# Low parts of every second weight unit on GpSimd from a2's keys to the output projection's first half, with the heads' scales one step and C's products two steps later

## The chip, the cores and the metric

The kernel runs on one core of a Trainium2 chip. The metric is the device time of one execution in microseconds (us), and the time of a kernel is the median of several runs. The engines are TensorE (PE; its weight loads are PEld), VectorE (DVE), ScalarE (ACT), GpSimd (POOL) and SyncE (SP), which here only issues DMAs.

## The reference

One decoder layer on x of 512 tokens and 2048 channels, in float32. A first RMSNorm and one input projection make the inputs of three token mixers, whose outputs go through one output projection and are added to x; then come a second RMSNorm and a SwiGLU block, added again.

```
proj = rms_norm(x) @ w_in                        # 2048 -> 3840 columns
A: 8 heads x 64, dilated sliding windows (128,1), (512,4), (2048,16), mixed by their softmax sums
B: u * sigmoid(gate) -> causal depthwise conv, 31 taps -> LayerNorm -> silu, 512 channels
C: 16 query heads x 64 over 2 kv heads, window 128, one learned sink per head
x  = x + concat(A, B, C) @ w_out                 # 2048 -> 2048
h2 = rms_norm(x)
x  = x + (silu(h2 @ w_gate) * (h2 @ w_up)) @ w_down
```

A and C normalise queries and keys per head before the scores.

## The kernel before, in words

**Products in three parts.** A float32 operand is split into a high part, the operand rounded to the matmul's type, and a low part, what the rounding left. Every product of a weight tile with the activations is then three matmuls (`mm3`, L321 to L324): high by high, high weights by low activations, low weights by high activations. The third one is the only reader of the low weights `wl`.

**Weight units.** The weights come in units of 128x1024. The input projection uses units 0 to 62: a projection's name in `PROJ` (such as `ak2`, the keys of A's head pair 2) takes two units from the fifth name on, and `ak2` begins with unit 35. The output projection takes units 63 to 94, its first half 63 to 78. `split_up_to` makes the parts two units ahead of their use: ACT casts the unit into the high part `wh` (L289), and a later subtraction of `wh` from the raw weights makes `wl` (recorded at L290; the profile puts it at L263, the helper that calls it). Which engine subtracts is the third field of the unit's entry in `works`; in the kernel before it is DVE for all 95 units.

```python
works.append((u, True, nc.vector))                                            # L167
(nc.vector.tensor_copy if u == 0 else nc.scalar.copy)(hi[:, :n], t[:, :n])    # L289
lows.append((eng.tensor_sub, lo[:, :n], t[:, :n], hi[:, :n].bitcast(F32)))    # L290
```

The raw weights, `wh` and `wl` each lie in SBUF. High and low parts have three buffers each, so the cast of unit u waits until PE has done with unit u-3. The raw buffer is given to a later load one unit after the subtraction was recorded.

**Steps.** The order of the work around the projections is set by `Ticks`: a list of functions that are due a number of steps later. A projection ticks after every second weight tile, that is after six matmuls (`project`, L538 to L550); the output projection's first half does the same, its second half ticks half as often. Every engine works through its instructions in the order in which they were recorded, so a function that is due one step later stands six matmuls later in PE's order and behind one more step of other work on DVE, ACT and POOL.

**Heads.** `head_scales` (L622) computes a projection's per-head scales: squares on ACT, a transposed sum on DVE, a small DRAM round trip on SP's queue, and three small operations on POOL (L655 to L657). Keys go on through a DVE transpose (L702), another round trip and a split; their tiles end in `wide`, `k`, `hi`, `lo`. `attention` (L793) then places a head: scores on PE (L814, L815), softmax on DVE and ACT, the flip (PE transposes of the weights: L850 in C, L916 in A), high and low parts of the flipped weights (ACT L856 and DVE L861 in C; ACT L922 and DVE L927 in A), and the products with the values (`weigh`, L940 with the high parts, L941 with the low parts). In C the flipped weights hold two blocks each, and POOL writes them apart with affine selects: `ph` from the high part, `pl` from the low one (L870, L873). `SD` enters only the earliest step of a head's scores:

```python
box["q at"] = ticks.now + SD + 3                                              # L668
return head_scales(b, name, then, home), ticks.now + SD + KD + 10             # L717, a key's step
t0 = max(ticks.now + ready, head_at[0], box["q at"] - s1, box["k at"], box["v at"] - at_v)   # L961
```

`C_TICKS` and `A_TICKS` hold a head's distances in steps, the last one (`we`) that from the split of the flipped weights to their products. A's heads are soft-maxed at L880 to L900 on DVE: the last operation before a flip is L900, which writes `a0e`, `a1e` and so on.

**Beside the heads** run the convolution's 31 taps for each of four channel tiles on DVE (L573, two SBUF inputs), one every 1.2 to 1.6 steps, and in the output projection the residual additions on DVE (`xr`, L1073), which also free the PSUM bank of an output tile; there are two such banks. POOL has, besides, the convolution's gate product (L564) and the scaling of values (L764).

**Later stages.** The SwiGLU block follows with its own order: weight sums on POOL (L172), low parts on DVE (L285, one input in PSUM), and products on PE (L1279 to L1282, L1544 to L1546).

Of the kernel before, what the change touches and what calls it, by code (L numbers as in the profile page):

```python
# [36 lines left out]
T_GLU = 14  # L37


SD, KD, VD, EV = 9, 6, 12, 1  # L40


C_TICKS = (1, 6, 2, 2, 2, 3, 5, 1, 4)
A_TICKS = (0, 8, 2, 1, 3, 1, 3, 1, 5)


PROJ = ("bu0 bg0 bu1 bg1 cv ck cq0 bu2 cq3 cq1 cq5 bu3 cq2 bg2 cq7 "
        "bg3 ak2 cq4 ak0 av0 cq6 ak1 aq0 av1 aq1 ak3 av2 aq2 av3 aq3").split()
ROWS = "c0 c1 c2 c4 c5 c3 c7 c6 a0 a1 b2 b1 b0 b3 a2 a3".split()

N_SLOTS = 73
# [65 lines left out]
def kernel(ctx: ExitStack, tc: tile.TileContext, xT, wi, wo, wgu, wd, cst_in, outT):  # L117
    nc = tc.nc
# [30 lines left out]
    entries, works = [], []  # L149
# [14 lines left out]

    for u, unit in enumerate(units):
        entries.append((RAW_PLAIN[(u - 2) % len(RAW_PLAIN)], u, [unit]))
        works.append((u, True, nc.vector))  # L167

    def plus(to, a, b, n, buf=None):
        def go():  # L170
# [622 lines left out]
    def attention(kind, box, mix, mi, heads):  # L793
        ready, every, step, s1, sx, s2, fl, ev, we = C_TICKS if kind == "c" else A_TICKS

        if mi in ROWS[-2:]:
            fl, we = fl + 2, we + 3
# [217 lines left out]
    ticks.after(t_ln + 12, ln_out, mix)  # L1015
    for n, row in enumerate(r for r in ROWS if r[0] == "b"):
        ticks.after(t_ln + 13 + n, split_mix, row)
# [4 lines left out]
    for name in PROJ[HEAD4:]:  # L1022
        kind, what, j = name[0], name[1], name[2:]
        if name == PROJ[-2]:
            for n, row in enumerate(ROWS[:8]):
                ticks.after(6 + n, split_mix, row)
# [27 lines left out]
    def load_x(i):  # L1054
        if i < KT:
            n = OUT_ORDER[0][i]
            xr[n] = slot(f"xr{n}")
            nc.sync.dma_start(xr[n], xT[n])
# [68 lines left out]
    late.append(True)  # L1127
    for n, row in enumerate(r for r in ROWS if r in mix and r not in m_hi):
        ticks.after(10 + 2 * n, split_mix, row)
    for half in range(2):  # L1130
        for i, n in enumerate(OUT_ORDER[half]):
# [4 lines left out]
            for kk in range(8):  # L1136
                k = 8 * half + kk
                row = ROWS[k]
                while row not in m_hi:
# [6 lines left out]
            if half == 0:  # L1146
                load_x(i + 2)
        for row in ROWS[8 * half:8 * half + 8]:
            if half == 0:
# [544 lines left out]
```

## Time and profile before

| | |
|---|---|
| median of 3 runs | 1844.88 us (1844.69 to 1844.89) |
| the profiled execution | 1845.39 us, of which 1843.6 us are the profile's span |
| PE busy | 1835.2 us (100% of the span) |
| DVE, ACT, POOL busy | 1445.8, 1312.1, 1026.2 us |
| granted TensorE clock | 1.0 over the span |
| chain that ended last, by engine | PE 95%, DVE 3%, DMA 1% |

In order of time the span has the input projection with the heads (to about 389 us), the output projection (to about 580 us), the SwiGLU block's first products (to about 1418 us) and its second ones. A row of the timeline gives an instruction's start, its duration, engine, line, operation and operands; in square brackets stands how long its engine was idle before it and what ended that. A matmul's row is longer than the distance to the next one, since they overlap: the distance from start to start tells whether PE was held up. A row of the waits gives the waiting instruction, what it waited for, the total, the number of times and the longest.

### The profile page before, as it was taken

What the parts mean: (1) busy time and instruction counts of PE and PEld (TensorE: products, weight loads), DVE (VectorE), ACT (ScalarE), POOL (GpSimd) and SP (SyncE); (2) the same over time, 40 slices, a digit from 0 to 9 for tenths busy, and PEclk for the clock granted to TensorE, in tenths of its full rate; (3) what the DMA queues carried; (4) which work ended last, traced back from release to release, by engine and by line L of the source; (5) the groups of instructions that cost most, each with busy time, mean ns of one, the idle gap of its engine ahead of it and who ended that gap; (6) DMA issues with size and microseconds to landing.
All of it is one profiled execution on the core that took longest, in us unless ns stands there. A gap on an engine that the chain in (4) does not pass through costs nothing.

```text
span 1843.6 us, 26502 instructions
## 1 busy us (share of the span) xinstructions
PE 1835.2 (100%) x8314; PEld 1522.4 (83%) x8314; DVE 1445.8 (78%) x2063; ACT 1312.1 (71%) x1784; POOL 1026.2 (56%) x790
## 2 busy tenths in 40 slices
PE   9999999999999999999999999999999999999998
PEld 7888888888888888888888888888888888888887
DVE  6789988997689877778777787777777777777777
ACT  6345554553458788888888888888887778777775
POOL 0126644110003557886788767878676558776552
PEclk9999999999999999999999999999999999999999
DMA  7353345353343457677867778677687679877735
GB/s 276 87 150 93 87 121 153 107 161 116 124 149 103 115 151 191 188 213 182 225 187 200 201 188 226 181 209 199 182 273 258 204 225 295 257 254 260 240 119 110
DMA packets 398924, 334.61 MB, mean 181 GB/s; under 512 B 184256, under 2 KB 326720, under 8 KB 398784
## 3 DMA queue, kind: packets, MB, share of 16 engines
q1 hardware_dynamic: 398208, 332.14, 62.3%
q8 instruction: 66, 1.08, 0.3%
q10 hardware_dynamic: 576, 0.79, 0.1%
q14 instruction: 74, 0.61, 0.1%
HBM read 258.46 MB, written 65.98 MB: 176 GB/s over the span
## 4 chain that ended last, share of the span: by engine, by line
PE 95%; DVE 3%; DMA 1%; issue 0%; ACT 0%; SPq 0%; POOL 0%; DVEq 0%; POOLq 0%; ACTq 0%
PE out L1281 15%; PE out L1279 15%; PE out L1282 15%; PE out L1544 7%; PE out L1546 7%; PE out L1545 7%; PE o L322 3%; PE o L323 3%; PE o L324 3%; PE cq L322 2%; PE cq L324 2%; PE cq L323 2%; PE in L324 1%; PE in L323 1%; PE in L322 1%; PE aq L322 1%
## 5 line engine op out<-in xcount | busy, mean ns | idle before, releaser
L1279 PE MATMUL out<-wh,h 128*128 128x512 f32 x1232 | 479.2, 389 | 0.0
L1281 PE MATMUL out<-wl,h 128*128 128x512 f32 x1232 | 479.2, 389 | 0.0
L1282 PE MATMUL out<-wh,h 128*128 128x512 f32 x1232 | 479.2, 389 | 0.0
L1279 PEld LDWEIGHTS out<-wh,h 128*128 128x128 f32 x1232 | 231.2, 188 | 48.1
L1282 PEld LDWEIGHTS out<-wh,h 128*128 128x128 f32 x1232 | 231.2, 188 | 48.0
L1281 PEld LDWEIGHTS out<-wl,h 128*128 128x128 f32 x1232 | 231.2, 188 | 47.9
L1545 PE MATMUL out<-wl,a 128*128 128x512 f32 x620 | 240.4, 388 | 0.1
L1544 PE MATMUL out<-wh,a 128*128 128x512 f32 x620 | 240.4, 388 | 0.0
L1546 PE MATMUL out<-wh,a 128*128 128x512 f32 x620 | 240.3, 388 | 0.0
L289 ACT CAST wh<-w 128x1024 fp32r<-128x1024 f32 (+2 forms) x94 | 96.9, 1031 | 121.6 <-PE o L323 48.0
L1554 DVE TENSOR_TENSOR y<-y,out 128x512 f32<-128x512 f32 x192 | 128.5, 684 | 47.8 <-PE out L1546 46.1
L263 DVE TENSOR_TENSOR wl<-w,wh 128x1024 fp32r<-128x1024 f32 (+2 forms) x95 | 115.0, 1211 | 30.9 <-ACT wh L289 27.9
L1545 PEld LDWEIGHTS out<-wl,a 128*128 128x128 f32 x620 | 116.4, 188 | 24.5 <-DVE wl L285 0.5
L1546 PEld LDWEIGHTS out<-wh,a 128*128 128x128 f32 x620 | 116.4, 188 | 23.8
L1544 PEld LDWEIGHTS out<-wh,a 128*128 128x128 f32 x620 | 116.4, 188 | 23.8
L573 DVE SCALAR_TENSOR_TENSOR y<-bu,cst,y 128x511 f32<-128x511 f32 (+14 forms) x120 | 92.0, 767 | 1.3
L322 PE MATMUL o<-mh_c,wh 128*128 128x512 f32 x128 | 51.1, 399 | 0.2 <-DVE xr L1073 0.2
L322 PE MATMUL cq<-hh,wh 128*128 128x512 f32 x128 | 50.3, 393 | 0.0
L324 PE MATMUL o<-mh_c,wl 128*128 128x512 f32 x128 | 50.0, 391 | 0.0
L323 PE MATMUL o<-ml_c,wh 128*128 128x512 f32 x128 | 50.0, 390 | 0.0
L323 PE MATMUL cq<-hl,wh 128*128 128x512 f32 x128 | 49.9, 390 | 0.0
L324 PE MATMUL cq<-hh,wl 128*128 128x512 f32 x128 | 49.9, 390 | 0.0
(2351 smaller groups left out, 4766.5 us busy)
## 6 DMA issues: line engine op xcount, KB each, us to landing
od<-a SPq DMA_DIRECT2D x154, 256.0 KB
a<-od SPq DMA_DIRECT2D x154, 256.0 KB
w<-in_wi SPq DMA_DIRECT2D x58, 512.0 KB
w<-in_wo SPq DMA_DIRECT2D x32, 512.0 KB
x<-in_xT SPq DMA_DIRECT2D x16, 256.0 KB
xr<-in_xT SPq DMA_DIRECT2D x16, 256.0 KB
x2d<-xr SPq DMA_DIRECT2D x16, 256.0 KB
z<-x2d SPq DMA_DIRECT2D x64, 64.0 KB
```

Of the source, the lines that this page charges most:

```text
L263: fn(*args)
L289: (nc.vector.tensor_copy if u == 0 else nc.scalar.copy)(hi[:, :n], t[:, :n])
L322: nc.tensor.matmul(out, wh, xh, start=start, stop=False)
L323: nc.tensor.matmul(out, wh, xl, start=False, stop=False)
L324: nc.tensor.matmul(out, wl, xh, start=False, stop=stop)
L1279: nc.tensor.matmul(b, x[:, high], wh[:, s], start=c == f == 0 and q in (7, 1, 5, 2), stop=False, skip_group_check=True)
L1281: nc.tensor.matmul(b, x[:, high], wl[:, s], start=False, stop=False, skip_group_check=True)
L1282: nc.tensor.matmul(b, x[:, low], wh[:, s], start=False, stop=c == f == 1, skip_group_check=True)
L1544: nc.tensor.matmul(b[:, lo:hi], x[:, high], wh[:, s], start=start, stop=False, skip_group_check=True)
L1545: nc.tensor.matmul(b[:, lo:hi], x[:, high], wl[:, s], start=False, stop=False, skip_group_check=True)
L1546: nc.tensor.matmul(b[:, lo:hi], x[:, low], wh[:, s], start=False, stop=last, skip_group_check=True)
L1554: getattr(eng, op)(t, t, src)
```

## The change

Units 35, 37 and so on to 77, which are 22 of the 44 units from the first of `ak2` to the last of the output projection's first half, get their low part from GpSimd instead of VectorE. `SD` becomes 10, so that scores are placed one step later after their projection. The last distance of `C_TICKS` becomes 6, so that C's products stand two more steps behind the split.

```diff
-SD, KD, VD, EV = 9, 6, 12, 1
+SD, KD, VD, EV = 10, 6, 12, 1
-C_TICKS = (1, 6, 2, 2, 2, 3, 5, 1, 4)
+C_TICKS = (1, 6, 2, 2, 2, 3, 5, 1, 6)
+POOL_LOWS = (35, 79)
...
-        works.append((u, True, nc.vector))
+        works.append((u, True, nc.gpsimd if POOL_LOWS[0] <= u < POOL_LOWS[1] and u % 2 else nc.vector))
```

One line is added above all others that the text names, so lines from L49 on have a number one higher in the changed kernel (L263 becomes L264).

Three places show what moves. On PE, at the products of head pair 1 of C (`c1o`), the six rows ahead and the first of the products, before:

```order
L322 MATMUL cq_1740<-hh_410,wh_1674 128x512
L323 MATMUL cq_1740<-hl_411,wh_1674 128x512
L324 MATMUL cq_1740<-hh_410,wl_1675 128x512
L322 MATMUL cq_1740<-hh_435,wh_1674 128x512
L323 MATMUL cq_1740<-hl_436,wh_1674 128x512
L324 MATMUL cq_1740<-hh_435,wl_1675 128x512
L940 MATMUL c1o_1867<-c1ph_1790,cv_745 128x256
L941 MATMUL c1o_1867<-c1pl_1803,cv_745 128x256
```

and now:

```order
L323 MATMUL bg_1885<-hh_160,wh_1728 128x512
L324 MATMUL bg_1885<-hl_161,wh_1728 128x512
L325 MATMUL bg_1885<-hh_160,wl_1729 128x512
L323 MATMUL bg_1885<-hh_186,wh_1728 128x512
L324 MATMUL bg_1885<-hl_187,wh_1728 128x512
L325 MATMUL bg_1885<-hh_186,wl_1729 128x512
L941 MATMUL c1o_1918<-c1ph_1786,cv_745 128x256
L942 MATMUL c1o_1918<-c1pl_1808,cv_745 128x256
```

The products stood in the projection `cq2` and now stand in the next one, `bg2`: 18 projection matmuls later, of which 6 come from `SD` (scores and flip moved by them too) and 12 from `C_TICKS`. Every head of C moved in this way; A's scores, flips and products moved by 6 as long as projections run.

On POOL, at the second head of C's pair 2, the end of its high parts `c2ph`, its low parts `c2pl`, and the scale of the keys `ak2`, before:

```order
L870 AFFINE_SELECT c2ph_2376<-c2hp_2356 128x2x128
L873 AFFINE_SELECT c2ph_2376<-c2hp_2356 128x128
L870 AFFINE_SELECT c2pl_2398<-c2lp_2371 128x2x128
L873 AFFINE_SELECT c2pl_2398<-c2lp_2371 128x2x128
L870 AFFINE_SELECT c2pl_2401<-c2lp_2371 128x2x128
L873 AFFINE_SELECT c2pl_2401<-c2lp_2371 128x128
L695 MEMSET ak2wide 128x24
L655 TENSOR_TENSOR ak2wide<-ak2t 128x8
```

and now:

```order
L871 AFFINE_SELECT c2ph_2383<-c2hp_2354 128x2x128
L874 AFFINE_SELECT c2ph_2383<-c2hp_2354 128x128
L264 TENSOR_TENSOR wl_2365<-w_1914,wh_2364 128x1024
L696 MEMSET ak2wide 128x24
L656 TENSOR_TENSOR ak2wide<-ak2t 128x8
L657 TENSOR_TENSOR ak2wide<-ak2wide,c_531 128x8
L658 TENSOR_TENSOR ak2wide<-ak2wide,nhalf 128x8
L871 AFFINE_SELECT c2pl_2413<-c2lp_2378 128x2x128
```

The low part of unit 41 and the keys' scale now stand ahead of the head's low parts, which C's products wait for.

On DVE, inside the softmax of A's first pair (`a0`, second head), where unit 57's low part stood, before:

```order
L883 SCALAR_TENSOR_TENSOR a0d_3100<-a0d_3100,aq0r 128x1
L263 TENSOR_TENSOR wl_3553<-w_3129,wh_3552 128x1024
L927 TENSOR_TENSOR a0pl_3598<-a0t_3537,a0ph_3574 128x512
L573 SCALAR_TENSOR_TENSOR y_2941<-bu_1447,cst,y_2941 128x490
L896 SCALAR_TENSOR_TENSOR a0e_3588,a0d_3100<-a0e_3588,mult_a 128x384
```

and now:

```order
L884 SCALAR_TENSOR_TENSOR a0d_3089<-a0d_3089,aq0r 128x1
L574 SCALAR_TENSOR_TENSOR y_2936<-bu_1429,cst,y_2936 128x490
L635 TENSOR_REDUCE ak3p<-ak3sq 128x4x4
L955 TENSOR_TENSOR mix_c_3465<-mix_c_3465,c6o_3540 64x512
L928 TENSOR_TENSOR a0pl_3607<-a0t_3549,a0ph_3588 128x512
L574 SCALAR_TENSOR_TENSOR y_2936<-bu_1429,cst,y_2936 128x489
L897 SCALAR_TENSOR_TENSOR a0e_3600,a0d_3089<-a0e_3600,mult_a 128x384
```

Unit 57's low part is gone from DVE there, and since the head stands one step later, two operations of the projections' and C's own chains and the tap of the next step (the second L574) now come ahead of its second half. SP's order of DMAs did not change.

## The prediction

> **What bounds the kernel now.** I read the page first: which engine fills the span.
>
> ```profile
> PE 1835.2 (100%) x8314; PEld 1522.4 (83%) x8314; DVE 1445.8 (78%) x2063; ACT 1312.1 (71%) x1784; POOL 1026.2 (56%) x790
> ```
>
> PE is busy from end to end, and the change neither removes nor adds a matmul. So it can win only what PE waits between units 35 and 78, and it loses whatever new wait it brings there. The waits of PE, in total, times and longest:
>
> ```profile
> PE c1o L941 <- POOL c1pl L873: 0.8, 2, 0.5
> PE a0t L916 <- DVE a0e L900: 0.3, 1, 0.3
> PE o L322 <- DVE xr L1073: 0.2, 1, 0.2
> PE a1t L916 <- DVE a1e L900: 0.2, 1, 0.2
> ```
>
> Matmuls overlap, so these rows understate a wait; the distance from start to start gives it. PE's timeline at both heads of `c1o`, from the first product to the next projection matmul:
>
> ```profile
> 183.55 0.28 PE L940 MATMUL c1o<-c1ph,cv 128*128 128x256 f32 x1
> 184.34 0.39 PE L941 MATMUL c1o<-c1pl,cv 128*128 128x256 f32 x1 [0.52 <-POOL c1pl L873]
> 185.37 0.39 PE L941 MATMUL c1o<-c1pl,cv 128*128 128x256 f32 x1 [0.29 <-POOL c1pl L873]
> 185.77 0.45 PE L322 MATMUL cq<-hh,wh 128*128 128x512 f32 x1
> ...
> 195.41 0.28 PE L940 MATMUL c1o<-c1ph,cv 128*128 128x256 f32 x1
> 196.30 0.45 PE L322 MATMUL bg<-hh,wh 128*128 128x512 f32 x1
> ```
>
> The same eight products took 2.22 us with POOL's `c1pl` late and 0.89 us without: 1.33 us. The three others, all behind DVE:
>
> ```profile
> 345.23 0.49 PE L916 MATMUL a0t<-ident,a0e 128*128 128x128 f32 x3
> 346.00 0.33 PE L916 MATMUL a0t<-ident,a0e 128*128 128x128 f32 x1 [0.28 <-DVE a0e L900]
> 374.21 0.49 PE L916 MATMUL a1t<-ident,a1e 128*128 128x128 f32 x3
> 374.88 0.33 PE L916 MATMUL a1t<-ident,a1e 128*128 128x128 f32 x1 [0.17 <-DVE a1e L900]
> 402.23 0.39 PE L814 MATMUL a2s<-ak2h,aq 128*128 128x512 f32 x1
> 402.46 0.39 PE L815 MATMUL a2s<-ak2l,aq 128*128 128x512 f32 x1
> 403.05 0.47 PE L322 MATMUL o<-mh_c,wh 128*128 128x512 f32 x1 [0.20 <-DVE xr L1073]
> ```
>
> Undisturbed matmuls of 512 columns stand 0.23 us apart (402.23 to 402.46), so the output tile came 0.36 us late. A transpose of 128 columns takes some 0.11 us from start to start, an estimate from the eight products above (0.89 us); three would have ended at 345.55 and 374.54, so the fourth came 0.45 and 0.34 us late. That makes 1.15 us, and with `c1o` 2.5 us: what the change can win at most. The reason for the last three stands in DVE's busy time of the windows around A's first two pairs:
>
> ```profile
> 320.00:340.00 20.00, 18.55 (x49) 1.00 0.48 128
> 340.00:360.00 20.00, 19.48 (x53) 1.00 0.32 81
> 360.00:380.00 20.00, 19.32 (x48) 1.00 0.42 121
> ```
>
> DVE is full at 57.35 of 60 us, and A's flips have no slack there: the second flips of both pairs already wait.
>
> **The change part by part.** *C's products two steps later.* A step is six matmuls, 6 x 0.23 = 1.4 us, so the products get 2.8 us against their low parts. The wait at `c1o` was 0.52 + 0.29 us of idle time and at most 1.33 us in all; 2.8 us cover it. This head stands ahead of the first moved unit on POOL, so nothing new comes in front of its first half: **-1.3 us**. What follows the products (the heads' outputs) is read only in the output projection, long after.
>
> *Scores one step later.* Scores, softmax, flip and products move together, so no distance inside a head changes; heads' scales get 1.4 us more before they are read. On a full DVE the head also stands behind one more step of taps and other work, which takes back about what the step gives: 0, and from -1 to +1 us.
>
> *Low parts on POOL.* Over these units the low parts cost DVE:
>
> ```profile
> L263 DVE TENSOR_TENSOR wl<-w,wh 128x1024 fp32r<-128x1024 f32 x43 | 53.3, 1240 | 8.6 <-ACT wh L289 5.8 <-PE c4t L850 2.7
> ```
>
> 22 x 1.24 = 27 us leave DVE's queue. What they cost on POOL, and what they do to DVE, the same kind of operation shows where POOL first adds weights, in POOL's and DVE's timeline:
>
> ```profile
> 551.19 2.45 POOL L172 TENSOR_TENSOR w('s', 'u0A')_5703<-w('21', 'u0A')_5494,w('11', 'u0A')_5547 128x1024 f32<-128x1024 f32 x1 [68.71 <-DVE wl L263]
> ...
> 550.97 0.42 DVE L1123 TENSOR_TENSOR h<-ta,h 128x256 fp32r<-128x256 f32 x1
> 551.31 2.62 DVE L1123 TENSOR_TENSOR h<-h,h 128x256 fp32r<-128x256 f32 x1
> ```
>
> POOL takes 2.45 us for it. The same DVE operation takes 0.42 us just before and 2.62 us while POOL works: 551.31 + 2.62 = 553.93, that is 0.29 us behind POOL's end at 553.64. A DVE operation with two SBUF inputs therefore waits until POOL's is through. So a moved unit saves DVE 1.24 us and costs it between 0 and 2.45 us, by how soon such an operation is next in DVE's queue. Unit 57 as the example: ACT's cast, DVE's two taps and its low part, and PE's first matmul that reads it:
>
> ```profile
> 333.37 1.07 ACT L289 CAST wh<-w 128x1024 fp32r<-128x1024 f32 x1
> 334.40 0.72 DVE L573 SCALAR_TENSOR_TENSOR y<-bu,cst,y 128x492 f32<-128x492 f32 x1
> 335.88 0.73 DVE L573 SCALAR_TENSOR_TENSOR y<-bu,cst,y 128x491 f32<-128x491 f32 x1
> 338.87 1.23 DVE L263 TENSOR_TENSOR wl<-w,wh 128x1024 fp32r<-128x1024 f32 x1
> 347.11 0.39 PE L324 MATMUL aq<-hh,wl 128*128 128x512 f32 x1
> ```
>
> The cast ends at 334.44, POOL can start behind the first tap at 335.12 and would end at 337.57; the second tap, due at 335.88, waits 1.7 us. Less the 1.24 us saved, DVE is 0.45 us later. I take 1.6 us per unit, near this row, since taps stand some 1.5 us apart here; four moved units (55, 57, 59, 61) lie ahead of the last flip that has no slack, so DVE is 4 x (1.6 - 1.24) = 1.4 us later there, of which the stall passes on about 1.2 us: **+1.2 us**. The bounds are 4 x (0 - 1.24) = -5 us on DVE, where PE can win only the 0.45 + 0.34 us of the two flips, and 4 x (2.45 - 1.24) = +4.8 us.
>
> *The rest of the output projection's first half.* Units 63 to 77 do the same beside the residual additions, whose one late case cost 0.36 us at 403.05, and beside A's last two pairs. Their flips have slack, as the end of the first one's softmax on DVE and its flip on PE show (4.8 us):
>
> ```profile
> 400.57 0.48 DVE L900 TENSOR_SCALAR a2e<-a2e,a2d 128x512 f32<-128x512 f32 x1
> 405.89 0.49 PE L916 MATMUL a2t<-ident,a2e 128*128 128x128 f32 x3
> ```
>
>  I take **+0.2 us**, between -0.36 (it goes) and +1.2 us (one more unit's 2.45 - 1.24 us comes through).
>
> *PE's own need of the low parts.* Unit 57 is needed at 347.11, 9.5 us behind POOL's end as worked out above. So the subtraction itself is covered unless POOL is held up by most of two units; if that cover goes, each late unit costs PE its lateness in full.
>
> *What is queued behind it on POOL.* A moved unit stands ahead of affine selects and keys' scales, and DVE's transpose L702 waits for the latter. The fullest stretch is this one, with POOL's last low part of `c2`'s second head, the end of the keys' scale behind it, and PE's first need:
>
> ```profile
> 200.00:240.00 40.00, 40.00 (x212) 34.15 (x211) 37.97 (x74) 24.90 (x59) 27.10 (x42) 1.00 0.27 74
> ...
> 231.21 1.29 POOL L873 TENSOR_SCALAR_AFFINE_SELECT c2pl<-c2lp 128x128 fp32r<-128x128 f32 x1
> 233.45 1.64 POOL L657 TENSOR_TENSOR ak2wide<-ak2wide,nhalf 128x8 f32<-128x8 f32 x1
> 236.71 0.28 PE L941 MATMUL c2o<-c2pl,cv 128*128 128x256 f32 x1
> ```
>
> POOL is busy 27.1 of 40 us here; units 37, 39 and 41 add 3 x 2.45 = 7.4 us, and it still fits. At `c2` the head's low parts ended at 232.50; unit 41 (2.45 us) and the scale (from 232.50 to 235.09, 2.6 us) now come first: 237.5. The need moves from 236.71 by 3 x 1.4 to 240.9. So 3.4 us are left: 0, and at most the half of a microsecond on the few heads of this kind.
>
> Sum: -1.3 + 0 + 1.2 + 0.2 = **+0.1 us**. Against the profiled execution, 1845.39 us (a span of 1843.6 and 1.8 around it), this is 1845.5; that execution lay 0.5 us above the median of the runs, 1844.88, so the forecast for the median is **1845.0 us**.
>
> **The rivals.** *Slower: POOL's subtractions hold up DVE for their whole length.* Place: DVE between 318 and 380 us, ahead of `a0t` and `a1t`. It decides once a moved unit holds DVE for more than about 2.2 us: 4 x (2.45 - 1.24) = 4.8 us there and 1.2 us at the output tiles, less 1.3 us at `c1o`: +4.7 us, 1849.6. For it: the 2.62 us row, taps that follow each other without a gap, and a DVE with no idle time to make it up. Against it: operations with an input in PSUM lie between the taps. The Trainium skill, page "SBUF — State Buffer", section "SBUF: two separate sides", says that VectorE with two SBUF inputs and GpSimd share a port pair as an exclusive lock, held for the whole instruction, so that the loser blocks fully; by that rule the moved work costs DVE more than it saves wherever such an operation is next, and the row of 2.62 us agrees. Chance 0.20, with the case that POOL's queue makes C's products late (price: POOL twice as slow, some 1.5 us on each of four heads, 1849).
>
> *Better: DVE does get its 27 us.* If POOL's subtractions fall beside operations with a PSUM input, all four waits go: 1844.9 - 2.5 = 1842.4. For it: the low parts also made DVE wait 8.6 us for ACT's cast and for PE, in the row of L263, and half of that goes too. Against it: unit 57's row. Chance 0.25.
>
> *It does not do what it says:* a wait on POOL is replaced by the same wait on DVE, `c1o` still late because `c1lp` is. Then nothing changes but the DVE term: 1846. It is inside the forecast's range. The forecast itself has 0.52; more than 2.5 us can be won only by something that I do not see, 0.03.
>
> **How the numbers follow.** About 0.2%, 3.7 us, is what a measurement of this kernel can tell from no change. The forecast and the better case both lie within it: 0.52 + 0.25 = 0.77, of which I give 0.02 to the slower edge, since the bounds of the DVE term and of the output tiles together reach past it, and keep 0.75 within. Slower takes the first rival and that edge, 0.22; faster by over 3.7 us is 0.03. The range goes from the better case, 1842.4, less 0.4 us for the distance of a single execution from the median, to the price of the slower one: 1842.0 to 1849.6.
>
> **What would show it.** Right: PE's waits no longer name `c1pl`; `a0t` and `a1t` still wait for DVE, by about 1 us in all more than before; DVE's taps beside a POOL L264 last up to 2.5 us; POOL's L264 rows last 2.4 to 3 us and end over 5 us ahead of the L325 that reads them. Wrong: PE waiting for POOL at L325 or L942; the flips of A without any wait; the stretch of 320 to 380 us with idle time on DVE; or a difference outside 180 to 500 us.

## The result, and the profile after

The changed kernel took 1848.86 us in the median of 10 runs (1847.10 to 1850.31), the kernel before on the same chip 1844.63 us (10 runs): a ratio of 1.0024, interval 1.0015 to 1.0033, or 4.2 us more. The forecast was 1845.0 us and its range 1842.0 to 1849.6.

The profiled executions differ by less, 1847.10 against 1845.39 us, because of their first microseconds. PE's timeline at the first products, before and then after:

```profile
5.30 2.08 PE L516 MATMUL in<-hh,wh 128*128 128x512 f32 x4 [0.59 <-ACT hh L402]
```

```profile
5.37 1.20 PE L517 MATMUL in<-hh,wh 128*128 128x512 f32 x4 [0.87 <-ACT hh L403]
```

Four matmuls span 2.08 us in one and 1.20 in the other. Some ten matmuls stand 0.43 us apart here in the execution of the kernel before, which costs it 2 us, long ahead of the first thing that the change moves; the executions of either kernel spread by about as much or more. So kernels are compared below by a second number too: the time from one and the same early matmul (of the input projection's first tiles, at 28 to 30 us) to the last one, less the same in the kernel before. For the changed kernel that is **+3.65 us**. It all arose before 500 us. This number rests on one execution of each kernel. By the ratios in the table below, every version stands 0 to 1.5 us higher against the kernel before than by it (the changed one 4.4 us), so the profiled execution of the kernel before probably took a little longer than most; where two other versions are compared, that falls out.

Where it went stands in PE's waits of the changed kernel (its five longest; total, times, longest):

```profile
PE a0t L917 <- DVE a0e L901: 3.5, 1, 3.5
PE idle L349 <- DVE nhalf L353: 1.1, 1, 1.1
PE in L517 <- ACT hh L403: 0.9, 1, 0.9
PE sides L1510 <- DVE y L1524: 0.6, 1, 0.6
PE lv L473 <- DVE lnv L413: 0.4, 1, 0.4
```

The waits at `c1o`, `a1t` and the output tile are gone. One at `a0t` has grown from 0.3 to 3.5 us, and one at the LayerNorm's transposes (`lv`) is new. PE's timeline at `a0t` shows that the wait isn't all:

```profile
343.75 0.49 PE L917 MATMUL a0t<-ident,a0e 128*128 128x128 f32 x3
347.76 0.33 PE L917 MATMUL a0t<-ident,a0e 128*128 128x128 f32 x1 [3.53 <-DVE a0e L901]
...
348.40 0.40 PE L323 MATMUL aq<-hh,wh 128*128 128x512 f32 x1
348.63 0.40 PE L324 MATMUL aq<-hl,wh 128*128 128x512 f32 x1
...
349.68 0.63 PE L324 MATMUL aq<-hl,wh 128*128 128x512 f32 x1
350.10 0.63 PE L325 MATMUL aq<-hh,wl 128*128 128x512 f32 x1
```

The fourth transpose is 3.69 us late by the distance from start to start. From 349.25 on matmuls stand 0.43 us apart instead of 0.23, until 352.5; together they lose 1.6 us. The windows of that stretch (length, busy PE, PEld, DVE, ACT, POOL, granted clock, DMA share and GB/s) carry it as a clock of 0.91, beside a DVE that is as full as before:

```profile
320.00:340.00 20.00, 20.00 (x106) 16.99 (x105) 19.56 (x48) 12.04 (x19) 9.24 (x12) 1.00 0.34 97
340.00:360.00 20.00, 16.47 (x76) 13.68 (x75) 19.51 (x48) 6.31 (x10) 6.04 (x6) 0.91 0.35 93
360.00:380.00 20.00, 20.00 (x100) 16.80 (x99) 18.75 (x44) 13.53 (x24) 5.08 (x2) 1.00 0.37 103
```

So one place costs 5.3 us. DVE's and POOL's timelines tell what came first:

```profile
342.44 1.21 DVE L264 TENSOR_TENSOR wl<-w,wh 128x1024 fp32r<-128x1024 f32 x1
343.57 2.81 DVE L574 SCALAR_TENSOR_TENSOR y<-bu,cst,y 128x488 f32<-128x488 f32 x1
346.30 0.68 DVE L897 SCALAR_TENSOR_TENSOR a0e<-a0e,mult_a 128x512 f32<-128x512 f32 x1
...
347.22 0.49 DVE L901 TENSOR_SCALAR a0e<-a0e,a0d 128x512 f32<-128x512 f32 x1
```

```profile
343.49 2.37 POOL L264 TENSOR_TENSOR wl<-w,wh 128x1024 fp32r<-128x1024 f32 x1 [6.53 <-ACT wh L290]
```

POOL starts unit 59's subtraction 0.08 us ahead of a tap, and the tap lasts 2.81 us instead of 0.72. The softmax of `a0` is next on DVE, and PE waits for its end.

The page's sums give the price of all 22 units. Its first line, and the groups of L264 on DVE and POOL:

```profile
PE 1834.2 (99%) x8314; PEld 1522.1 (82%) x8314; DVE 1458.5 (79%) x2041; ACT 1313.9 (71%) x1784; POOL 1083.6 (59%) x812
```

```profile
L264 DVE TENSOR_TENSOR wl<-w,wh 128x1024 fp32r<-128x1024 f32 (+2 forms) x73 | 88.1, 1208 | 18.2 <-ACT wh L290 16.5 <-DMA w<-in_wi 1.5 <-PE c0t L851 0.2
L264 POOL TENSOR_TENSOR wl<-w,wh 128x1024 fp32r<-128x1024 f32 x22 | 56.5, 2566 | 100.1 <-ACT wh L290 100.1
```

DVE has 22 operations less, 26.9 us by this line (115.0 before), and yet is busy 12.7 us more (1445.8 before). Holds have thus added 39.6 us to its other operations, **1.8 us for each moved unit**, against 1.22 us saved (the two distances alone change DVE's sum by only 0.7 us).

### The profile page after: what moved, and what is told of

The parts are those of the page before. It is cut to its first block, busy times and chain, and to the rows that moved or that the text cites. A ratio compares the mean times of both kernels' runs of the same rounds, so it can differ in the third digit from the quotient of the medians.

```text
span 1845.4 us, 26519 instructions
## 1 busy us (share of the span) xinstructions
PE 1834.2 (99%) x8314; PEld 1522.1 (82%) x8314; DVE 1458.5 (79%) x2041; ACT 1313.9 (71%) x1784; POOL 1083.6 (59%) x812
## 3 DMA queue, kind: packets, MB, share of 16 engines
q8 instruction: 66, 1.08, 0.2%
## 4 chain that ended last, share of the span: by engine, by line
PE 73%; DVE 1%; DMA 0%; issue 0%; SPq 0%; ACT 0%; DVEq 0%
PE out L1283 15%; PE out L1280 15%; PE out L1282 15%; PE out L1546 7%; PE out L1545 7%; PE out L1547 7%; PE o L323 2%; PE o L325 2%; PE o L324 2%; DVE y L1555 0%; DVE wl L286 0%; DVE z L1454 0%; DVE lnv L413 0%; DMA out_T<-z 0%; DVE y L1524 0%
## 5 line engine op out<-in xcount | busy, mean ns | idle before, releaser
L264 POOL TENSOR_TENSOR wl<-w,wh 128x1024 fp32r<-128x1024 f32 x22 | 56.5, 2566 | 100.1 <-ACT wh L290 100.1
L574 DVE SCALAR_TENSOR_TENSOR y<-bu,cst,y 128x511 f32<-128x511 f32 (+14 forms) x120 | 104.3, 869 | 1.3
L264 DVE TENSOR_TENSOR wl<-w,wh 128x1024 fp32r<-128x1024 f32 (+2 forms) x73 | 88.1, 1208 | 18.2 <-ACT wh L290 16.5
L325 PE MATMUL o<-mh_c,wl 128*128 128x512 f32 x128 | 50.0, 391 | 0.0
L325 PE MATMUL cq<-hh,wl 128*128 128x512 f32 x128 | 49.9, 390 | 0.0
```

The lines of the kernel that those rows point to most:

```text
L264: fn(*args)
L325: nc.tensor.matmul(out, wl, xh, start=False, stop=stop)
L574: nc.vector.scalar_tensor_tensor(yconv[j][:, i:], hconv[j][:, :T - i], c, yconv[j][:, i:], op0=ALU.mult, op1=ALU.add)
```

## The experiments

All times in us. The last column is the comparison from 30 us on; "waits" are lost microseconds from start to start of PE's late matmuls in the profiled execution (the matmul behind a late one stands another 0.1 us late, which is not counted).

| kernel | median | ratio to before, interval | waits at A's flips and others | from 30 us on |
|---|---|---|---|---|
| changed | 1848.86 | 1.0024, 1.0015 to 1.0033 | a0t 3.69, half rate 1.6, lv 0.53 | +3.65 |
| unit 59 on DVE | 1846.17 | 1.0015, 1.0005 to 1.0024 | a0t 1.86, a1t 0.92, lv 0.51 | +1.37 |
| units 55 to 61 on DVE | 1844.57 | 1.0005, 0.9996 to 1.0014 | a0t 0.99, a1t 0.50, lv 0.55 | +0.06 |
| even units | 1847.92 | 1.0021, 1.0013 to 1.0030 | a0t 1.08, a1t 3.01, lv 0.55 | +3.02 |
| copies on POOL | 1843.67 | 1.0001, 0.9992 to 1.0009 | a0t 1.12, lv 0.54 | -0.41 |
| only POOL | 1851.23 | 1.0039, 1.0026 to 1.0052 | c1o 1.13, c5o 2.07, c6o 0.75, a0t 0.57, a1t 2.78 | +5.90 |
| both distances | 1844.95 | 1.0006, 0.9997 to 1.0015 | a0t 0.97, a1t 0.50, lv 0.54 | +0.03 |
| only scores' step | 1843.60 | 1.0001, 0.9992 to 1.0010 | c6o 0.21, a0t 1.04, a1t 0.63, lv 0.54 | +0.05 |
| only C's products | 1848.30 | 1.0025, 1.0016 to 1.0035 | c6o 0.76, a0t 2.55, half rate | +4.55 |
| C's products, flips a step later | 1848.00 | 1.0023, 1.0014 to 1.0032 | c6o 0.76, a0t 0.69, a1s 2.23, a0o 0.92 | +3.58 |
| changed, flips two steps later | 1847.99 | 1.0022, 1.0013 to 1.0031 | a0o 2.73, half rate, a1o 1.08, lv 0.53 | +4.06 |
| chains on DVE | 1852.17 | 1.0046, 1.0033 to 1.0060 | a0t 4.12, half rate, a1t 2.62 | +7.03 |
| both distances with room | 1841.69 | 0.9994, 0.9985 to 1.0003 | none | -2.26 |

**Which units cost.** One back on DVE, four back, and the even units in place of the odd ones:

```diff
-nc.gpsimd if POOL_LOWS[0] <= u < POOL_LOWS[1] and u % 2 else nc.vector
+nc.gpsimd if POOL_LOWS[0] <= u < POOL_LOWS[1] and u % 2 and u != 59 else nc.vector
+nc.gpsimd if POOL_LOWS[0] <= u < POOL_LOWS[1] and u % 2 and not 55 <= u <= 61 else nc.vector
+nc.gpsimd if POOL_LOWS[0] <= u < POOL_LOWS[1] and u % 2 == 0 else nc.vector
```

> Only unit 59 goes back to DVE; the other 21 moved units stay on POOL. Theory (one place): unit 59's subtraction on POOL holds one tap and with it the end of a0's second softmax, so PE's fourth transpose comes 3.7 us late, and the ten matmuls that follow the wait run at half rate, 1.6 us more. Without it the wait at a0t falls under 0.7 us, no matmul near 350 us stands 0.43 us from the next, and the median is about 1848.9 - 5 = 1844 us. Rival (DVE has too much work everywhere between 320 and 380 us): one unit of 2.4 - 1.24 us more or less moves the wait by about 1.2 us at most; the median stays at 1847.5 to 1849.

> Units 55, 57, 59 and 61, all that lie between 316 and 367 us, go back to DVE; 18 units stay on POOL. Both theories expect the waits at a0t and a1t to be as short as before the change (0.5 us and less). One place: no better than with unit 59 alone back, 1843.5 to 1844.5 us. Too much work on DVE: clearly better than with unit 59 alone back, by 3 us or more.

Unit 59 alone takes 1.83 us off the wait at `a0t`, and no matmul runs at half rate behind it in the profiled execution; the other three units take 0.87 us more there and 0.42 at `a1t`. The waits, first without unit 59 and then without all four:

```profile
PE a0t L917 <- DVE a0e L901: 1.7, 1, 1.7
...
PE a1t L917 <- DVE a1e L901: 0.8, 1, 0.8
```

```profile
PE a0t L917 <- DVE a0e L901: 0.8, 1, 0.8
...
PE a1t L917 <- DVE a1e L901: 0.3, 1, 0.3
```

Neither theory had it whole. Unit 59 is the dearest, 2.3 of the 3.65 us (at `a0t` it is 1.83 and the half rate's 1.6, of which `a1t` takes back 0.9, since PE comes there earlier); the other three cost 1.3 us together, and the remaining 18 cost nothing (+0.06 against +0.03 with no unit on POOL at all). That the four units cost is clear by the ratios too, whose intervals do not overlap. How much of it is unit 59's rests on the profiled execution, 1845.16 us, which is among the fastest of eleven (1844.94 to 1848.91): the ratios' intervals with and without unit 59 overlap.

> The changed kernel with the even units from 36 to 78 on POOL instead of the odd ones: as many, 22 low parts. DVE then has no low part of its own right ahead of a0's second flip (unit 58 stood there), and unit 59's comes behind it in DVE's order; POOL does unit 58 when its cast is done, well ahead of the flip. Theory (the loss is one place: a subtraction on POOL beside the last operations ahead of a flip): a0t waits 1 to 1.7 us, no half rate, 1845 to 1846.5 us. Rival (so many subtractions on POOL cost DVE as much wherever they lie): a0t and a1t together 3 us and more, half-rate matmuls behind, 1847 to 1849 us.

The theory of one place falls. There was no half rate, and `a0t` waited as little as it expects, but `a1t` waits 3.0 us in both heads together:

```profile
PE a1t L917 <- DVE a1e L901: 2.6, 2, 1.5
...
PE a0t L917 <- DVE a0e L901: 0.8, 2, 0.5
```

So with either choice of units a flip is hit as long as units between 316 and 380 us are moved; which one depends on the choice.

**What holds DVE.** POOL copies instead of subtracting:

```diff
-lows.append((eng.tensor_sub, lo[:, :n], t[:, :n], hi[:, :n].bitcast(F32)))
+lows.append((eng.tensor_copy, lo[:, :n], t[:, :n]) if eng is nc.gpsimd else (eng.tensor_sub, ...))
```

> The changed kernel, but POOL only copies the raw weights of the 22 moved units into the low part (one input instead of two; the low parts of these units are left out). It need not wait for the cast, so it may start earlier. Theory (POOL's operation with two SBUF inputs holds a DVE operation with two SBUF inputs until it is through): taps beside the copies last at most 0.3 us longer, DVE is rid of 22 x 1.24 us, a0t's wait is under 0.5 us, and the time is 1842.4 to 1843.7 us. Rival (any POOL operation of that size holds DVE, or DVE is simply late): taps beside the copies last 2 us and more, a wait of 2 us and more at a0t, 1847 to 1849 us.

The time is as the theory has it, its reason is wrong, and `a0t` still waits 1.12 us, not under 0.5. DVE's and POOL's timelines of this kernel:

```profile
342.83 1.53 DVE L897 SCALAR_TENSOR_TENSOR a0e<-a0e,mult_a 128x512 f32<-128x512 f32 x1
```

```profile
342.56 1.25 POOL L264 CAST wl<-w 128x1024 fp32r<-128x1024 f32 x1 [8.35 <-PE av L325]
```

An operation with one input holds DVE as well: L897 lasts 1.53 us instead of 0.68. It only ends sooner, after 1.25 us instead of 2.4: the hold lasts until POOL's operation is through. The Trainium skill, page "SBUF — State Buffer", section "SBUF: two separate sides", says that whichever of the two takes the shared port pair first has it for its whole instruction; these rows agree. By the profile's sums DVE is busy 1429.9 us in this kernel, so a copy holds it for 0.5 us on average, where a subtraction held it for 1.8. The copies are shorter (1.20 against 2.57 us in the mean), and they need not wait for the cast and so meet other operations; no run separates the two.

**The two distances.** Only the low parts on POOL, both distances alone, and each of them alone:

```diff
-SD, KD, VD, EV = 10, 6, 12, 1
-C_TICKS = (1, 6, 2, 2, 2, 3, 5, 1, 6)
-POOL_LOWS = (35, 79)
+SD, KD, VD, EV = 9, 6, 12, 1                # only POOL; only C's products
+C_TICKS = (1, 6, 2, 2, 2, 3, 5, 1, 4)       # only POOL; only the scores' step
+POOL_LOWS = (0, 0)                          # the three without POOL
```

> The low parts on POOL, with the distances of the kernel before. C's products wait for low parts queued behind POOL's subtraction: worked out with 4.2 us less of distance, c2's second head is 0.8 us late and a few heads like it, 1 to 3 us in all. At A's flips the theory of one place expects a wait of 2 to 4 us with half-rate matmuls behind it only if a POOL subtraction again falls beside the last tap ahead of a flip: 1847 to 1853 us in all. Rival (the distances are to blame for the wait at a0t): no long wait at a0t, 1844.6 to 1847 us.

With the old distances POOL makes C's products late, by 2.07 us at `c5o`, 0.75 at `c6o` and less at `c4o`; `c2`'s head, for which the wait was worked out, is not late. PE's timeline at `c5o`:

```profile
214.41 0.28 PE L941 MATMUL c5o<-c5ph,cv 128*128 128x256 f32 x1
216.08 0.39 PE L942 MATMUL c5o<-c5pl,cv 128*128 128x256 f32 x1 [1.39 <-POOL c5pl L874]
```

So the distances are what keeps POOL's queue out of PE's way. At A it is `a1t` here that waits, 2.78 us.

> The two distances changed, no low part on POOL. One place: c1o's wait is gone (1.3 us), a1t's and the output tile's too if they come from the step, and nothing new appears: 1844.6 - 1.3 to 2 = 1842.6 to 1843.3 us. Rival (the later scores put two more DVE operations ahead of a0's second softmax, and these cost the flip its time): a wait at a0t of 1 to 3.7 us stays without POOL, 1844 to 1848 us.

> Of the change only C's products two steps later; scores at the old distance, no low part on POOL. With both distances the trace showed c1o's wait gone (1.1 us) and the output tile's (0.36), but a0t and a1t 0.5 and 0.2 us later and a new wait of 0.5 us at the LayerNorm's transposes (lv). Theory: c1o's gain is C's distance alone, and the three new delays are the scores' step. Then here no wait at lv, a0t and a1t as before the change (0.45 and 0.34 us), the output tile's 0.36 us back, and 1.1 us less than before, about 1843.2 us. Rival: C's later products cause the new delays; then they are here too and the time is that of before, 1844.2 to 1844.9 us.

> Of the change only the scores' step; C's products at the old distance, no low part on POOL. Theory (of the run with both distances, the later waits at a0t, a1t and lv come from the scores' step, c1o's gain from C's): c1o waits 1.1 us as before the change, a0t 0.97, a1t 0.50, lv 0.54 us, the output tile not: 0.9 us more than before, 1843.8 to 1845.4 us. Rival (these delays need C's later products, whose buffers are held longer, as in the run with C's products alone): a0t 0.45, a1t 0.34 and no wait at lv; the time of before, within 0.4 us.

With both distances `c1o`'s gain is given back: `a0t` waits 0.97 us, `lv` 0.54, and the sum is +0.03. C's products alone cost 4.55 us, which no theory had (0.5 of it at one wait for ACT in the SwiGLU block, far behind the change). DVE's timeline there:

```profile
329.88 0.69 DVE L682 TENSOR_TENSOR aq1l<-aq1raw,aq 128x512 fp32r<-128x512 f32 x1 [4.57 <-POOL c6pl L874]
```

DVE stands idle for 4.57 us until POOL has finished `c6pl`, which `aq1l` isn't computed from: so it is probably a buffer that it waits for (both tiles, and the low part that POOL reads for `c6pl`, come from one pool of buffers, `slot` in the kernel), which no run shows by itself. POOL's row in turn waited for PE's products of `c6o`, and these are late by their own distance. The scores' step alone already removes the wait at `c1o` and makes the later waits at `a0t` and `lv`; the rival, that they need C's products, falls. With C's products alone `c1o` doesn't wait either: either distance is enough for that, and my theory that the gain is C's alone falls too.

**Room for A's flips.** The changed kernel with flips two steps later and the products in place; C's products alone with one step:

```diff
-A_TICKS = (0, 8, 2, 1, 3, 1, 3, 1, 5)
+A_TICKS = (0, 8, 2, 1, 3, 1, 5, 1, 3)       # changed, two steps
+A_TICKS = (0, 8, 2, 1, 3, 1, 4, 1, 4)       # C's products alone, one step
```

> The changed kernel with its low parts on POOL, and A's flips two steps (2.8 us) later, the products in place. Theory (unit 59 makes one softmax end 3.7 us late against its flip, the rest follows from that): a0t waits 0.9 us, no matmul behind it runs at half rate, the time falls by 2.8 + 1.6 to about 1844.5 us. Rival (DVE stays late, and the wait moves on to the next reader): a wait at L942 of a0o for the low parts of the flipped weights, or at a1t, takes its place, 1846 to 1849 us.

The rival, word for word. DVE is late, and the next reader waits:

```profile
PE a0o L942 <- DVE a0pl L928: 2.6, 1, 2.6
...
PE a1o L942 <- DVE a1pl L928: 0.9, 1, 0.9
```

> As the run with C's products alone, and A's flips one step later with the same place of the products. Theory (A's flips merely have no slack): 1.4 us of room take the waits at a0t and a1t away (0.45 + 0.34 us): about 1842.4 us. Rival (the work behind the flip has no room either): the low parts of the flipped weights come too late for products that are one step nearer, PE waits for DVE at L942 of a0o or a1o, 1843.2 us or more.

Again the rival, and more: `a1s` waits twice for DVE's additions (1.36 and 0.87 us). It shares the late `c6o` with the run before, so it doesn't tell whether room alone would have sufficed.

**Idle PE and the half rate.** Chains on DVE take POOL's place:

```diff
+for _ in range({'a0': 8, 'a1': 8}.get(name, 0) if h == 1 and u == len(us) - 1 else 0):
+    nc.vector.tensor_scalar(e[:, :T], e[:, :T], 1.0, None, op0=ALU.mult)
```

> The kernel before, nothing on POOL, and two chains of plain DVE multiplications by 1.0 (some 0.4 us each) ahead of a flip: 8 of them behind the second softmax of a0, 8 behind that of a1. It leaves POOL out of the stall. Theory (idle time of PE alone brings the half rate): a0t waits 0.45 + 8 x 0.4 = 3.6 us, the matmuls behind it stand 0.43 us apart for some 3 us as in the changed kernel (1.6 us more), a1t then waits about 0.34 + 3.2 - 0.45 - 1.6 = 1.5 us and nothing behind it runs at half rate: 5 to 6.5 us more than before, about 1850 us. Rival (the half rate has to do with POOL's work beside it): the same waits, matmuls 0.23 us apart right behind them, 1.6 us less.

The half rate comes without POOL, behind the wait at `a0t`, and not behind the one at `a1t` (PE's timeline; the flip's line is L919 here):

```profile
347.92 0.33 PE L919 MATMUL a0t<-ident,a0e 128*128 128x128 f32 x1 [3.96 <-DVE a0e L903]
...
349.68 0.63 PE L324 MATMUL aq<-hl,wh 128*128 128x512 f32 x1
350.10 0.63 PE L325 MATMUL aq<-hh,wl 128*128 128x512 f32 x1
...
380.59 0.33 PE L919 MATMUL a1t<-ident,a1e 128*128 128x128 f32 x1 [2.45 <-DVE a1e L903]
380.68 0.48 PE L323 MATMUL aq<-hh,wh 128*128 128x512 f32 x1
380.99 0.40 PE L324 MATMUL aq<-hl,wh 128*128 128x512 f32 x1
381.22 0.40 PE L325 MATMUL aq<-hh,wl 128*128 128x512 f32 x1
```

So a wait of PE brings it without any low part on POOL; why the second wait did not stays open. The kernel costs 7.0 us, more than the 5 to 6.5 expected, since `a1t` waits 2.62 us and not 1.5.

**A version without these waits.** The two distances, no low part on POOL, A's flips one step later with the products in place; for the last two pairs the products one step earlier.

```diff
-A_TICKS = (0, 8, 2, 1, 3, 1, 3, 1, 5)
-POOL_LOWS = (35, 79)
+A_TICKS = (0, 8, 2, 1, 3, 1, 4, 1, 4)
+POOL_LOWS = (0, 0)
...
-            fl, we = fl + 2, we + 3
+            fl, we = fl + 1, we + 3
```

> Both distances as in the change, no low part on POOL, and A's flips one step later with the products in place; for the last two pairs flips in place and products one step earlier. Against the run with both distances alone the theory (A's flips have no slack against DVE, and the LayerNorm's transposes wait because a3's products come a step later) takes away the waits at a0t (0.97 us), a1t (0.50) and lv (0.54): 2 us less, 1842.3 to 1843 us, under the kernel before. Rival (as where the flips got two steps with POOL at work: the lateness goes on to the flipped weights' low parts, or to a buffer): PE waits for DVE at L942 of a0o or a1o, or at a1s, 0.7 to 1.5 us each; 1844 to 1847 us.

All PE waits that the profile lists in this kernel:

```profile
PE idle L349 <- DVE nhalf L353: 1.1, 1, 1.1
PE in L517 <- ACT hh L403: 0.8, 1, 0.8
PE sides L1510 <- DVE y L1524: 0.6, 1, 0.6
```

Between the first products and the last outputs the profile lists no wait any more. From 30 us on it is 2.26 us shorter than the kernel before and 5.9 us shorter than the changed one. Its median is 1.2 us under that of the kernel before, and the interval of the ratio (0.9985 to 1.0003) still holds 1, so a gain over the kernel before is not shown by the times; over the changed kernel it is.

## Why the prediction was right or wrong

The range held the time, but only by its upper part, which the slower rival had set; the likeliest value was 3.9 us too low, and the difference of 0.24% lies just over the 0.2% within which I expected it. Two terms of the sum failed, the scores' step by some 1.3 us and the low parts up to 380 us by 2.4 us. Step by step:

**What bounds the kernel: right.** PE is full, the change won and lost nothing outside 180 to 500 us, and the last version shows that all the named waits could be won.

**C's products, -1.3 us: the wait goes, but two steps alone are dear.** The 1.33 us were there: the eight products that took 2.22 us take 0.88 in the changed kernel (185.90 to 186.78). Either distance removes the wait by itself. C's two steps add nothing to the scores' step without POOL, and cost 4.55 us by themselves, probably since buffers are held longer; the prediction asked only who reads the products, not what waits for their buffers. With POOL's low parts on, the distances are needed: without them C's products lose 3 us.

**Scores one step later, 0 us: the smaller step that failed.** The run with this step alone measures +0.05, but that contains `c1o`'s gain, and both distances together, forecast at -1.3 us, measure +0.03. "A step gives 1.4 us and DVE takes it back" hides +0.59 at `a0t`, +0.29 at `a1t`, +0.21 at `c6o` and +0.54 at `lv`, where a3's products come a step later and push the LayerNorm's sums on DVE, 1.6 us in all, and against them -1.33 and -0.36 us at `c1o` and the output tile. I had looked for what is late next at C, not at the end of the stage.

**Low parts up to 380 us, +1.2 us: the larger step that failed.** Measured is the changed kernel less both distances alone, 3.65 - 0.03 = 3.6 us. The working took 1.6 us for each of four units and gave each its 1.24 us back. The price of a unit was near: ahead of `a0t`'s late transpose unit 55 holds DVE for 1.64 us, unit 57 for 1.54 and unit 59 for 2.09, by the tap above and these two rows (0.29 and 0.16 us undisturbed):

```profile
317.26 1.93 DVE L897 SCALAR_TENSOR_TENSOR a0e<-a0e,mult_a 128x128 f32<-128x128 f32 x1 [0.60 <-ACT a0e L890]
332.54 1.70 DVE L884 SCALAR_TENSOR_TENSOR a0d<-a0d,aq0r 128x1 f32<-128x1 f32 x1
```

Mis-sized was unit 59, which gets nothing back there. In DVE's queue its subtraction stands behind the end of `a0`'s softmax; with unit 59 back on DVE the softmax ends at 345.82 us, and the subtraction comes here:

```profile
349.40 1.22 DVE L264 TENSOR_TENSOR wl<-w,wh 128x1024 fp32r<-128x1024 f32 x1
```

POOL does not stand in DVE's queue; it was idle for 6.53 us before, so it ran the subtraction when ACT's cast was done and met a tap that DVE's order put ahead of it. Three holds less two savings of 1.22 us make 2.8 us, and `a0t` waits 2.72 us longer than with both distances alone. The wait that unit 59 makes long enough brings the half rate, 1.6 us more, which the working didn't contain; against it the 0.50 us at `a1t` go. A row of matmuls at half rate was in the profile before: the first ones.

**Rest of the output projection, +0.2 us: near 0.** The 18 units outside 316 to 367 us cost 0.03 us, and the output tile's wait went.

**PE's own need and POOL's queue: right.** PE waits nowhere for POOL; POOL's low parts lie ready 4.3 us and more ahead of L325 (the "over 5 us" missed for one unit), and last 2.37 to 2.90 us.

**The rivals.** The slower one gave 1849.6 us by a hold of more than 2.2 us for each unit. The time came near for another reason: the holds ahead of `a0t` are 1.5 to 2.1 us and their mean over all units is 1.8, and the rest is the saving that unit 59 lacks and the half rate. The better one, "DVE does get its 27 us", is not what limits: with copies half as long DVE is 15.9 us less busy than before, and the time falls by 0.41 us only, since `a0t` still waits.

**What would show it.** Of the signs, `c1pl` is gone from the waits and taps last up to 2.9 us (2.5 were forecast). "About 1 us in all more" at `a0t` and `a1t` is 3.69 against 0.45 at the one, and none at the other, which comes after the delay.

## What to carry to other kernels

Work moved from a full engine to an idle one that shares its port costs the first engine up to the length of the second one's operation (here 1.8 of 2.57 us in the mean), at whatever instruction it meets, and it saves time only behind its old place in the queue: go through the deadlines one by one, and count a saving only where the old place lay ahead of them. Where a full engine feeds PE at every link of a chain, moving one link later passes the lateness on; here it took no POOL work and one step of room to make it vanish. A wait of some microseconds on PE can have a second price in the matmuls behind it.

## What of the hardware was not expected

- A wait of 3.5 us on PE is followed by about 3 us of matmuls 0.43 us apart, and waits of 2.6 and 2.4 us were too (`a0o` with flips two steps later, `a0t` with C's products alone, there by over 5 us of them); waits of 2.45 and 1.7 us were not. So length alone does not decide. The Trainium skill, page "TensorE: Matmul & The Clock Gate", section "Part 1: The HAM clock gate", speaks of a free-running window of about 3.4 us, which would explain that it varies, though waits shorter than that window sufficed here.
- DVE operations that read PSUM were not held by POOL: over the changed kernel L881 and L1074 last the same beside a POOL L264, while even L884, normally 0.16 us, lasts up to 2.2 us. An operation with one input in SBUF is held too (L901, 2.52 us with the low parts alone on POOL).
